# A masked prefix sum and a product: the last block comes last, in two parts, and is summed column group by column group

## The chip, the core and the metric

The kernel runs on one core of a Trainium2 chip. The metric is the device time of one execution in microseconds (us); smaller is better. TensorE multiplies matrices and writes to PSUM, VectorE and ScalarE work element by element, GpSimd fills tables, and SyncE and ScalarE issue the transfers between device memory and the on-chip memory (SBUF). Each engine has a queue of its own; semaphores tie them together.

## The reference

```
B, S, D = 8, 8192, 512
masked = x * (pos < lengths[:, None, None])
cs = np.cumsum(masked, axis=1)
mid_features = cs[arange(B), lengths // 2, :]
return matmul(mid_features[:, None, :], w).squeeze(1)
```

Only one row of each cumulative sum is used, so what is computed is, for each of the 8 sequences, the sum of its first n rows, n = min(length // 2 + 1, length), and then the product of the 8 sums (8x512) with w (512x512). Everything is float32. With the inputs drawn here n is 570, 2690, 256, 2057, 905, 3772, 3859 and 571 for sequences 0 to 7. In whole blocks of 512 rows that is 1, 5, 0, 4, 1, 7, 7 and 1 block, and a remainder of 58, 130, 256, 9, 393, 188, 275 and 59 rows. These are 26 blocks of 1 MB, some 3 MB of remainders, and 1 MB of w.

## The kernel before

**Tiling.** A block of 512 rows lies in SBUF as 128 partitions of four rows each (`(p g) d -> p g d`, 8 KB in one piece per partition). Four matmuls sum it: matmul j takes row j of every partition, and its weights (128 partitions by 8 columns) have ones in the column of the present sequence and zeros elsewhere. The four go to four column groups of the array, 32 columns apart, and each adds its 8 sums of 512 columns into partitions 32j to 32j+7 of the PSUM tile `s_ps`. In float32 each matmul shows as two records, so a block shows as eight.

**Stages.** VectorE first computes the row counts and a table of weights (`table`), in a chain of steps, each of which waits for the one before (`step`, L301 in the profile). Per sequence it copies that sequence's weights to `cur`. TensorE then goes through the sequences in pairs (`for q in range(2)`): it takes the weights and the remainder of the sequence (four matmuls), then its whole blocks (`add_block`). Ahead of each block but a sequence's first stand two bfloat16 matmuls into `idle_ps` (128x512), whose result nobody uses.

**Loads.** SyncE issues the whole blocks in order, into 6 buffers for even and 6 for odd sequences (`xt`, `NP = 6`). Before it fills a buffer again it waits until `s_sum`, which counts the sums made, has passed the one that last read it (`until`, L202). The very first block of sequence 0 goes to a tile of its own (`first`), before the lengths are known. ScalarE issues w and the remainders (`PARTS`: pieces of 256, 128, 64 rows and a last one of up to 64), into `rem`, one tile for even and one for odd sequences. `rem` has been zeroed by GpSimd (L289); ScalarE waits for that.

**End.** When all sums are made, VectorE copies `s_ps` to `s_sb` in two halves, ordered by column modulo 4 (L301, `s_sb<-s_ps`). Four matmuls with `fold` (L431) add the four groups and transpose at once: each takes 128 columns of `s_sb` as weights, and yields 128 columns of D on partitions by 8 sequences (`mf_ps`). Two copies bring them to `mf_sb`, and 16 matmuls multiply by w (L439) into `o_ps`. VectorE and ScalarE copy one half of the result each, and SyncE and ScalarE store them.

**Counts.** SyncE, ScalarE, VectorE and TensorE hold row counts in registers (`Counts`): they load the lengths from SBUF and compute with the queue's register instructions. Loops and conditions (`whole_blocks`, `Fori`, `If_cmp`) are branches on these engines' queues.

Of the kernel before, what the change touches and what calls it, by code (L numbers as in the profile page):

```python
# [16 lines left out]
def kernel(  # L17
# [15 lines left out]

    nc = tc.nc
# [5 lines left out]
    NP = 6  # L40
# [20 lines left out]
    def sem(name):  # L61
        return tc.alloc_semaphore(name)

    xt = sb("xt", [P, 2, NP, G, D])
    first = sb("first", [P, G, D])
# [3 lines left out]
    warm = sb("warm", [1, 1])  # L69
    n_i = sb("n_i", [1, B], I32)  # L70
    n_f = sb("n_f", [1, B])
    ones = sb("ones", [1, P])
    zb = sb("zb", [1, 32], BF16)
# [8 lines left out]
    first_w = sb("first_w", [P, B])  # L82
# [3 lines left out]
    zero = sb("zero", [1, D])  # L86
    fold_i = sb("fold_i", [P, B], I32)
    fold = sb("fold", [P, B])
    s_sb = sb("s_sb", [P, KC, P])
    mf_sb = sb("mf_sb", [P, KC, B])  # L90
# [3 lines left out]
    mf_ps = [ps(f"mf_ps{h}", [P, D]) for h in range(2)]  # L94
# [7 lines left out]
    s_w, s_first, s_len1, s_go, s_out = sem("w"), sem("first"), sem("len1"), sem("go"), sem("out")  # L102
# [7 lines left out]
    class Counts:  # L110


        def __init__(self, eng, ready, count, loaded=B):


            self.eng = eng
            self.raw = [eng.alloc_register(f"n_{eng.engine.name}_{i}") for i in range(2 * loaded)]
            self.regs = self.raw[::2]
            self.t = eng.alloc_register(f"t_{eng.engine.name}")
            eng.wait_ge(ready, count)  # L120
            eng.load(self.raw, lens1[:, :2 * loaded])
            self.pair = None
            if loaded < B:
                self.pair = eng.alloc_register(f"pair_{eng.engine.name}")
                eng.reg_mov(self.pair, 0)

        def without_first(self, base=None):

            alu, t, n = self.eng.reg_alu, self.t, self.rows(0)
            alu(t, n, 9, ALU.logical_shift_right)  # L130
            alu(t, t, 1, ALU.min)
            alu(t, t, 9, ALU.logical_shift_left)
            alu(n, n, t, ALU.subtract)
            if base is not None:
                alu(base, base, t, ALU.add)

            alu(n, n, 1, ALU.logical_shift_left)
            alu(n, n, 1, ALU.subtract)
            alu(n, n, 0, ALU.max)

        def rows(self, b):

            n = self.regs[b]
            self.eng.reg_alu(self.t, n, 1, ALU.logical_shift_right)
            self.eng.reg_alu(self.t, self.t, 1, ALU.add)
            self.eng.reg_alu(n, self.t, n, ALU.min)
            return n

        def next_pair(self):
            if self.pair is not None:  # L150

                self.eng.reg_alu(self.pair, self.pair, 4, ALU.add)
                self.eng.reg_alu(self.pair, self.pair, 2 * B - 4, ALU.min)
                self.eng.load(self.raw, lens1[:, ds(self.eng.snap(self.pair, min_val=0, max_val=2 * B - 4), 4)])
                return
            for to, of in zip(self.regs, self.regs[2:]):
                self.eng.reg_mov(to, of)

    def whole_blocks(eng, n, most, body, k=0):
# [5 lines left out]
    DVE_SEL, DVE_N, DVE_MASK = 2, 6, 28  # L165
# [6 lines left out]
        out=first[:], in_=xf[:BLK].rearrange("(p g) d -> p g d", g=G)  # L172
    ).then_inc(s_first, 16)
# [9 lines left out]
    def _(sp):  # L183
        ns = Counts(sp, s_len1, 16, loaded=2)
        sp.sem_inc(s_go, 1)
        base, at = sp.alloc_register("sp_base"), sp.alloc_register("sp_at")
        sp.reg_mov(base, 0)
        ns.without_first(base)

        items = sp.alloc_register("sp_items")  # L190
        sp.reg_mov(items, 2)
        until = [[sp.alloc_register(f"until{q}_{k}") for k in range(NP)] for q in range(2)]
        for u in until[0] + until[1]:
            sp.reg_mov(u, 1)
        with sp.Fori(0, B // 2):
            for q in range(2):
                n = ns.rows(q)
                sp.reg_alu(items, items, 1, ALU.add)

                def load_block(k):  # L200
                    sp.wait_ge(s_sum, until[q][k % NP])
# [275 lines left out]
```

## Time and profile before

| | |
|---|---|
| median of 14 runs | 88.89 us (87.97 to 89.81) |
| the profiled execution's own time | 88.54 us |
| its span, first to last instruction | 86.7 us |
| mean granted TensorE clock | 0.941 |
| moved by DMA | 31.29 MB, mean 361 GB/s |
| busy: TensorE matmuls, VectorE, ScalarE, GpSimd | 54.5, 10.6, 2.0, 4.4 us |
| issue of a whole block to its landing, median | 13.8 us |
| SyncE's waits for a sum before it fills a buffer again | 36.5 us in 10 waits |

The profile comes from one execution. Times in it count from the span's start; the 1.84 us between its span and its time lie outside. In a line of a timeline the columns are start, duration, engine (PE is TensorE, PEld its weight loads, DVE VectorE, ACT ScalarE, SPq SyncE's queue), line, operation, output <- inputs, shapes and count; in brackets the idle time of the engine before it and what ended that.

### The profile page before, as it was taken

To read this page: it belongs to the slowest core of one execution; us is meant where nothing else is said; L and a number is where in the kernel's file an instruction comes from. 1 tells how busy PE (TensorE), PEld (TensorE's weight loads), DVE (VectorE), ACT (ScalarE), POOL (GpSimd) and SP (SyncE) were. 2 spreads that over 40 slices of the span, in tenths; PEclk is the share of its full clock that TensorE was granted. 3 is DMA by queue.
4 is the path that set the end of the run, shared out by engine and by line. 5 is a ranking of instruction groups with operands and counts; after the bars stand their busy time and mean duration, and the time that the engine had idled before them with its cause. 6 is when DMAs were issued, how large, how long until landed. Compare 5 with 4: busy or idle time off the path is not lost. (4 is left out here: it accounts for less than half of the span.)

```text
span 86.7 us, 1383 instructions
## 1 busy us (share of the span) xinstructions
PE 54.5 (63%) x346; PEld 10.9 (13%) x350; DVE 10.6 (12%) x42; ACT 2.0 (2%) x4; POOL 4.4 (5%) x9
## 2 busy tenths in 40 slices
PE   0920251999994898059966199744995677448730
PEld 0220000121110211010200001100210011011520
DVE  3977600000000000000000000000000000000520
ACT  0000000000000000000004200000000000000020
POOL 5940000000000000000000000000000000000000
PEclk9999999999999999995799858997599999999999
DMA  2799999999999999999999999999999999990000
GB/s 30 321 408 291 374 404 423 416 431 423 419 415 420 423 419 419 416 396 424 423 419 417 417 425 423 423 423 423 423 416 416 423 423 423 423 389 15 0 0 11
DMA packets 4694, 31.29 MB, mean 361 GB/s; under 512 B 658, under 2 KB 674, under 8 KB 946
## 3 DMA queue, kind: packets, MB, share of 16 engines
q1 hardware_dynamic: 3762, 27.27, 76.7%
q10 hardware_dynamic: 928, 3.97, 11.8%
q14 instruction: 3, 0.02, 0.1%
q8 instruction: 1, 0.02, 0.1%
HBM read 31.23 MB, written 0.02 MB: 360 GB/s over the span
## 5 line engine op out<-in xcount | busy, mean ns | idle before, releaser
L381 PE MATMUL s_ps<-xt,cur 128*8 128x512 f32 x200 | 29.2, 650 | 14.8 <-PEq L108 14.7
L381 PE MATMUL s_ps<-rem,cur 128*8 128x512 f32 x64 | 12.3, 806 | 5.3 <-PEq L108 5.3
L415 PE MATMUL idle_ps<-idle 128*128 128x512 bf16 x30 | 9.8, 400 | 0.5 <-issue 0.3
L381 PEld LDWEIGHTS s_ps<-xt,cur 128*8 128x8 f32 x200 | 4.3, 90 | 30.4 <-issue 30.2
L355 DVE COPY cur<-table 128x40 f32<-128x40 f32 x8 | 1.4, 184 | 51.8 <-PE s_ps L381 51.8
L381 PE MATMUL s_ps<-first,first_w 128*8 128x512 f32 x8 | 1.9, 1042 | 4.0 <-DVE table L301 4.0
L415 PEld LDWEIGHTS idle_ps<-idle 128*128 128x128 bf16 x34 | 1.9, 98 | 15.6 <-issue 15.6
L381 PEld LDWEIGHTS s_ps<-rem,cur 128*8 128x8 f32 x64 | 1.8, 91 | 15.3 <-issue 15.2
L389 PE MATMUL s_ps<-zero 1*128 1x512 f32 x2 | 2.1, 1132 | 2.3 <-DVE ones L301 2.3
L289 POOL MEMSET rem<- 128x4096 f32 x1 | 3.5, 3511 | 0.0
L301 DVE COPY s_sb<-s_ps 128x256 f32<-128x256 f32 x2 | 0.8, 424 | 17.3 <-PE s_ps L381 17.3
L301 DVE TENSOR_SCALAR n_i<-lens 1x8 int32<-1x8 int32 x1 | 2.8, 2770 | 0.2 <-DMA lens<-in_lengths_dram 0.2
L275 ACT ACT_TABLE_LOAD x1 | 1.3, 1283 | 46.8 <-PE s_ps L381 46.8
L431 PE MATMUL mf_ps<-fold,s_sb 128*128 128x8 f32 x8 | 1.1, 260 | 0.5 <-DVE s_sb L301 0.5
L392 PE MATMUL n_ps<-n_f,ones 1*128 1x8 f32 x2 | 0.6, 368 | 1.2 <-DVE n_f L301 1.2
L278 ACT COPY o_sb<-o_ps 8x128 f32<-8x128 f32 x2 | 0.5, 258 | 35.0 <-PE o_ps L439 35.0
L431 PEld LDWEIGHTS mf_ps<-fold,s_sb 128*128 128x128 f32 x8 | 1.0, 190 | 1.5 <-DVE s_sb L301 1.5
L439 PE MATMUL o_ps<-wt,mf_sb 128*8 128x128 f32 x32 | 1.1, 273 | 0.0
L392 PEld LDWEIGHTS n_ps<-n_f,ones 1*128 1x128 f32 x2 | 0.5, 308 | 2.8 <-DVE n_f L301 2.8
L389 PEld LDWEIGHTS s_ps<-zero 1*128 1x128 f32 x2 | 0.5, 304 | 2.3 <-DVE ones L301 2.3
L439 PEld LDWEIGHTS o_ps<-wt,mf_sb 128*8 128x8 f32 x32 | 0.8, 89 | 0.0
L301 DVE COPY o_sb<-o_ps 8x128 f32<-8x128 f32 x2 | 0.6, 280 | 0.9 <-PE o_ps L439 0.8
(37 smaller groups left out, 6.7 us busy)
## 6 DMA issues: line engine op xcount, KB each, us to landing
xt<-in_x_dram SPq DMA_DIRECT2D x25, 1024.0 KB, 13.8
rem<-in_x_dram ACTq DMA_DIRECT2D x3, 512.0 KB, 7.1
wt<-in_w_dram ACTq DMA_DIRECT2D x1, 1024.0 KB, 6.4
first<-in_x_dram SPq DMA_DIRECT2D x1, 1024.0 KB, 8.2
rem<-in_x_dram ACTq DMA_DIRECT2D x3, 256.0 KB, 6.5
rem<-in_x_dram ACTq DMA_DIRECT2D x3, 128.0 KB, 6.5
rem<-in_x_dram ACTq DMA_DIRECT2D x3, 32.0 KB, 5.8
rem<-in_x_dram ACTq DMA_DIRECT2D x1, 64.0 KB, 6.2
```

The source lines that it names most:

```text
L275: act.copy(out=warm[:], in_=zero[:, :1])
L278: copy = act.copy(out=o_sb[1][:, j * P:(j + 1) * P], in_=o_ps[64 + 32 * j:64 + 32 * j + B, :P])
L289: pool.memset(rem[:], 0.0).then_inc(s_pool, 1)
L301: do(*args, **kw).then_inc(s_dve, 1)
L355: dve.tensor_copy(out=cur[:, b % 2], in_=table[:, b * WT:(b + 1) * WT]).then_inc(s_cur[b % 2], 1)
L381: return pe.matmul(s_ps[32 * j:32 * j + B], lhsT=weights, rhs=rows, start=False, stop=False, skip_group_check=True, tile_position=(0, 32 * j))
L389: pe.matmul(s_ps[:], lhsT=zero[:, :P], rhs=zero[:], start=True, stop=False, skip_group_check=True)
L392: pe.matmul(n_ps[:, :B], lhsT=ones[:], rhs=n_f[:], start=True, stop=True).then_inc(s_pe, 1)
L415: pe.matmul(idle_ps[:], lhsT=idle[:, :P], rhs=idle[:], start=True, stop=True)
L431: mm = pe.matmul(mf_ps[h][:, i * B:(i + 1) * B], lhsT=s_sb[:, 2 * h + i], rhs=fold[:], start=True, stop=True)
L439: mm = pe.matmul(o_ps[32 * j:32 * j + B, :P], lhsT=mf_sb[:, kc], rhs=wt[:, kc, j * P:(j + 1) * P], start=(kc == 0), stop=(kc == KC - 1), t ...
```

## The change

- **First block.** `first` is gone. Sequence 0's first block is loaded to the first of the `xt` buffers, still before the lengths are known, and is summed as that sequence's whole block, behind its remainder, with weights whose entry is zero where the sequence has fewer than 512 rows.
- **Last block.** If the last sequence has a whole block, its last one isn't among the blocks of the loop. SyncE issues it behind all others, into a tile `last` of its own and as two transfers, rows 0 and 1 and rows 2 and 3 of each partition, each with its own semaphore.
- **End.** After the loop `s_ps` is copied to `s_sb` as it stands, in two halves. Four matmuls with `fold` as weights (`add_column`) add the groups, matmul j for columns 128j to 128j+127, into partitions 32j to 32j+7 of `t_ps`. The last block is then added to the same tile: for each of its four rows four matmuls of 128 columns each. VectorE transposes `t_ps` in blocks of 32x32 into `t_sb`, in two instructions, and the product with w takes its weights from there.
- **Idle matmuls.** The pair (`keep_busy`) now also stands ahead of each sequence's remainder, ahead of the folds and ahead of the last block.
- **Buffers.** `NP` goes from 6 to 5.
- **Zeroing.** ScalarE zeroes the even half of `rem`, GpSimd the odd half, the latter once VectorE has made its tenth step. ScalarE's early `warm` copy, which came behind its loads, is gone.
- **Counts.** VectorE computes the rows per sequence for TensorE and itself into `blk_i` (five more steps); SyncE and ScalarE load the lengths by pairs (`Pairs`) and set their other registers before that.

```diff
-    NP = 6
+    NP = 5
...
-    class Counts:
+    class Pairs:
...
+        def step(self):
+
+            alu, top = self.eng.reg_alu, 2 * B - 4
+            alu(self.at, self.at, 4, ALU.add)
+            alu(self.at, self.at, top, ALU.min)
+            self.eng.load(self.raw, lens1[:, ds(self.eng.snap(self.at, min_val=0, max_val=top), 4)])
...
     nc.sync.dma_start(
-        out=first[:], in_=xf[:BLK].rearrange("(p g) d -> p g d", g=G)
-    ).then_inc(s_first, 16)
+        out=xt[:, 0, 0], in_=xf[:BLK].rearrange("(p g) d -> p g d", g=G)
+    ).then_inc(s_full[0][0], 16)
...
     @block.sync
...
+                    with sp.If_cmp(ns.at, 2 * B - 4, "IS_GE"):
+                        alu(has_last, n, 9, ALU.logical_shift_right)
+                        alu(has_last, has_last, 1, ALU.min)
+                        alu(last_at, has_last, 9, ALU.logical_shift_left)
+                        alu(n, n, last_at, ALU.subtract)
+                        alu(last_at, n, ~(BLK - 1), ALU.bitwise_and)
+                        alu(last_at, last_at, base, ALU.add)
...
+                def load_block(k):
+                    sp.wait_ge(s_sum, until[q][k % NP])
+                    alu(items, items, 1, ALU.add)
+                    sp.reg_mov(until[q][k % NP], items)
+                    if (q, k) == (0, 0):
+
+                        with sp.If_cmp(ns.at, 1, "IS_GE"):
+                            load(k)
+                    else:
+                        load(k)
...
+        with sp.If_cmp(has_last, 1, "IS_GE"):
+            from_rows = rows(sp, at, last_at, 0, BLK).rearrange("(p g) d -> p g d", g=G)
+            for h in range(2):
+                sp.dma_start(
+                    out=last[:, 2 * h:2 * h + 2], in_=from_rows[:, 2 * h:2 * h + 2]
+                ).then_inc(s_last[h], 16)
...
     @block.scalar
...
-        act.wait_ge(s_pool, 2)
+        act.memzero(rem[:, 0]).then_inc(s_zero[0], 1)
+        ns = Pairs(act, s_go, 1)
...
+                act.wait_ge(s_zero[q], 1)
                 act.wait_ge(s_sum, until[q])
...
-        act.wait_ge(s_dve, DVE_SEL)
-        act.copy(out=warm[:], in_=zero[:, :1])
...
-        pool.memset(rem[:], 0.0).then_inc(s_pool, 1)
         pool.memset(idle[:], 1.0).then_inc(s_pool, 1)
+        pool.wait_ge(s_dve, DVE_BLK)
+        pool.memset(rem[:, 1], 0.0).then_inc(s_zero[1], 1)
...
-        cols = s_ps[:].rearrange("p (i kc) -> p kc i", kc=KC)
         for h in range(2):
-            step(dve.tensor_copy, out=s_sb[:, 2 * h:2 * h + 2], in_=cols[:, 2 * h:2 * h + 2])
+            step(dve.tensor_copy, out=s_sb[:, 2 * P * h:2 * P * (h + 1)], in_=s_ps[:, 2 * P * h:2 * P * (h + 1)])
+        dve.wait_ge(s_pe, B + 3)
         for h in range(2):
-            dve.wait_ge(s_pe, B + 2 + h)
-            step(dve.tensor_copy, out=mf_sb[:, 2 * h:2 * h + 2].rearrange("p a b -> p (a b)"), in_=mf_ps[h][:, :2 * B])
+            step(dve.transpose, out=t_sb[:, 2 * h:2 * h + 2].rearrange("p k c -> p (k c)"),
+                 in_=t_ps[:, :P].rearrange("p (c k) -> p k c", k=KC)[:, 2 * h:2 * h + 2])
...
+        def keep_busy():
+
+            for _ in range(2):
+                pe.matmul(idle_ps[:], lhsT=idle[:, :P], rhs=idle[:], start=True, stop=True)
+
+        def add_column(j, weights, row, **kw):
+
+            return pe.matmul(t_ps[32 * j:32 * j + B, :P], lhsT=weights, rhs=row[:, P * j:P * (j + 1)],
+                             stop=False, skip_group_check=True, tile_position=(0, 32 * j), **kw)
...
-                pe.wait_ge(s_first, 16)
-                for j in range(G):
-                    mm = add(j, first_w[:], first[:, j])
-                mm.then_inc(s_sum, 1)
                 with pe.Fori(0, B // 2):
                     for q in range(2):
+                        keep_busy()
                         take(pe, s_cur[q], 1)
                         take(pe, s_rem[q], 16 * (len(PARTS) + 1))
...
-                for h in range(2):
-                    pe.wait_ge(s_dve, DVE_MASK + 1 + h)
-                    for i in range(2):
-                        mm = pe.matmul(mf_ps[h][:, i * B:(i + 1) * B], lhsT=s_sb[:, 2 * h + i],
-                                       rhs=fold[:], start=True, stop=True)
+                keep_busy()
+                for j in range(4):
+                    if j % 2 == 0:
+                        pe.wait_ge(s_dve, DVE_MASK + 1 + j // 2)
+                    mm = add_column(j, fold[:], s_sb, start=True)
+                mm.then_inc(s_pe, 1)
+                with pe.If_cmp(ns[B], 1, "IS_GE"):
+                    keep_busy()
+                    for g in range(G):
+                        if g % 2 == 0:
+                            pe.wait_ge(s_last[g // 2], 16)
+                        for j in range(4):
+                            mm = add_column(j, cur[:, 1, :B], last[:, g], start=False)
                     mm.then_inc(s_pe, 1)
+                with pe.Else():
+                    pe.sem_inc(s_pe, 1)
```

## The prediction

> **What bounds the kernel now.** I read the page's first two parts, then stretches of the span, then the timeline at both ends, then who waits for whom.
>
> ```profile
> span 86.7 us, 1383 instructions
> PE 54.5 (63%) x346; PEld 10.9 (13%) x350; DVE 10.6 (12%) x42; ACT 2.0 (2%) x4; POOL 4.4 (5%) x9
> DMA  2799999999999999999999999999999999990000
> ```
>
> Every compute engine has much idle time; the DMA row is at 9 from about 4 us to 78 us. The 31.29 MB are the bound, until the last slices, where nothing is moved any more. The columns of the next view are the stretch, its length, the busy time of the five engines, granted clock, DMA share, GB/s.
>
> ```profile
> 6.00:7.00 1.00, 0.21 (x2) 0.12 (x1) 0.52 (x7) 0.00 (x0) 0.00 (x0) 1.00 0.99 418
> 7.00:8.00 1.00, 0.00 (x0) 0.00 (x0) 0.83 (x6) 0.00 (x0) 0.00 (x0) 1.00 1.66 344
> 8.00:9.00 1.00, 0.00 (x0) 0.00 (x0) 0.83 (x6) 0.00 (x0) 0.00 (x0) 1.00 0.37 156
> 77.00:78.00 1.00, 0.90 (x9) 0.27 (x11) 0.00 (x0) 0.00 (x0) 0.00 (x0) 1.00 0.89 369
> 78.00:79.00 1.00, 1.00 (x12) 0.15 (x6) 0.00 (x0) 0.00 (x0) 0.00 (x0) 1.00 0.10 41
> ```
>
> The stream runs at about 420 GB/s, with one gap at 7 to 9 us, worth (420-344+420-156)/420 = 0.8 us: the 1 MB of `first` and of w are through, and the first block that SyncE issues after reading the lengths, at 5.08, isn't flowing yet. The end, from the timeline:
>
> ```profile
> 74.61 1.04 PE L381 MATMUL s_ps<-xt,cur 128*8 128x512 f32 x8 [0.90 <-PEq L108]
> 77.10 1.04 PE L381 MATMUL s_ps<-xt,cur 128*8 128x512 f32 x8 [1.45 <-PEq L108]
> 77.96 1.18 PE L381 MATMUL s_ps<-rem,cur 128*8 128x512 f32 x8
> 79.55 1.04 PE L381 MATMUL s_ps<-xt,cur 128*8 128x512 f32 x8 [0.41 <-PEq L108]
> 80.65 0.88 DVE L301 COPY s_sb<-s_ps 128x256 f32<-128x256 f32 x2 [17.25 <-PE s_ps L381]
> 81.13 1.07 PE L431 MATMUL mf_ps<-fold,s_sb 128*128 128x8 f32 x8 [0.54 <-DVE s_sb L301]
> 82.13 1.06 PE L439 MATMUL o_ps<-wt,mf_sb 128*8 128x128 f32 x32
> 83.26 0.59 DVE L301 COPY o_sb<-o_ps 8x128 f32<-8x128 f32 x2 [0.84 <-PE o_ps L439]
> ```
>
> At 77.10 TensorE sums the last block of sequence 6, at 77.96 the remainder of sequence 7, at 79.55 (0.14 after its landing, 13.8 us after issue at 65.58) the only whole block of sequence 7 (571 rows); then come copies, folds, product, copies. The start:
>
> ```profile
> 14.78 1.90 PE L381 MATMUL s_ps<-rem,cur 128*8 128x512 f32 x8 [2.66 <-PEq L108]
> 16.82 2.01 PE L381 MATMUL s_ps<-rem,cur 128*8 128x512 f32 x8 [0.15 <-PEq L108]
> 18.48 1.21 PE L381 MATMUL s_ps<-xt,cur 128*8 128x512 f32 x8
> 20.00 24.83 SPq L204 DMA_DIRECT2D xt<-in_x_dram  x12
> ```
>
> SyncE issues five blocks by 9.6, then needs a buffer whose sum ends at 19.69, and issues again at 20.00. The fifth of those blocks lands at 24.8 (15.6 after issue at 9.24); its data and the remainder beside it are through at about 23.5. So the stream is not broken there, but with little to spare.
>
> **The change part by part.** The profiled execution took 88.54 us: span 86.7 and 1.84 around it; the median is 88.89, 0.35 above. I add to the median.
>
> *Head, SyncE.* Some 16 register moves (0.05 each in the trace of its queue, 0.8) now stand ahead of the load of the lengths, which waited until 2.12 anyhow; moving from 1.7 to 2.6 it starts 0.4 late. Behind it 14 moves and the split of the first block go (0.9), a comparison, a branch taken past the load and more register work come in (0.4 to 0.5). The first block of sequence 1 is issued about 0.0 to 0.2 earlier than 5.08: nothing, bounds -0.3 and +0.3. The gap at 7 to 9 us stays.
>
> *Head, the zeroing of `rem`.* Half goes to ScalarE, behind its table load (1.28 in the row of L275). Its own price is not shown: the lower bound is ScalarE's copies, 0.19 for one column and 0.26 for 128, so 0.5 ns a column and 1.3 for 2048; the upper VectorE's slope, (424-175)/240 = 1.04 ns a column, 2.3. I take 1.76, half of GpSimd's row of 3.51, the same work. From 1.8 it ends at 1.8+1.28+1.76 = 4.85 (4.4 to 5.4); GpSimd's memset, which it replaces, ended at 4.87. So the first remainder is issued at about 6.65 and lands 8.0 later, as before. [...] The other half stays on GpSimd (1.76, behind VectorE's tenth step) and is needed at 7.9 only. VectorE's first read of the lengths took 2.77, ending with GpSimd's memset; that shrinks, five steps of 0.19 come in, but TensorE waits for the remainder until 14.7 either way: nothing.
>
> *Start, TensorE.* `first` was summed at 10.22 to 12.1, while the remainder was on its way. Now that block is summed behind the remainder, in time that counts, with two idle matmuls ahead of each remainder. At the slow clock a pass of four matmuls starts every 0.80, at the full one every 0.43 (the granted clock reads 1.00 all along here, so only the durations tell); the fast passes begin at 18.5, 3.7 after 14.78. From 14.78: remainder 1.60, block 1.60, idle 0.43+0.22 (the clock turns here), remainder 0.86, block of sequence 1 0.43+0.59: end at 20.5 instead of 19.69. SyncE issues at 20.8 to 20.9 instead of 20.00. Is the stream dry by then? The block issued at 5.08 into a stream about to end flowed at 7.66, 2.6 later, and cost a ramp of 0.8; by that row 20.9+2.6 = 23.5 against 23.4, so 0.1+0.8 = 0.9 lost. w's transfer, issued at 0.89, moved its first packet at 1.94, 1.05 later; by that row 22.0, and nothing is lost. I take 0.5, the middle, since each row has a defect (the first fell among other issues, the second met idle engines); bounds 0 and 0.9 in this clock phase. [...]
>
> *Buffers 12 to 10, plus `last`.* The sixth and seventh block of sequences 5 and 6 now wait for the sums of blocks 1 and 2 of the same sequence. Sequence 5's first block lands at 42.9 and is summed by 44.3; four blocks of 2.48 are then still on their way. `last` is issued behind sequence 6's seventh block, as two transfers (one more issue of 0.34 on SyncE's queue) at about 66.5 against 65.58, to land at 79.4. Hidden by 10 us of queued transfers; without that cover a block would cost up to 2.5.
>
> *End.* Count from L, the landing of sequence 6's last block (76.96 before). Before, o_sb starts at L+6.30. Now:
> - its sum starts at L+0.14. Two idle matmuls come ahead of the remainder (0.54; the step from one block to the next with them is 1.51): remainder from L+1.65 to L+2.69 (was to L+2.18).
> - copies to s_sb, 0.42 each: L+2.75 to L+3.63. TensorE's queue, after a sequence's last sum, needs 1.4 of branches and register work (79.59 to 81.01 before); from L+1.8 it is through at L+3.3, two idle matmuls then, so the folds (four of N=128, 0.22 as in the product) go at L+3.9.
> - a second pair of idle matmuls, with nothing to cover it, stands behind the folds: 0.54, `last` from L+4.7.
> - `last`'s halves land at L+1.3 to L+2.6: two microseconds earlier. So the wait on them costs nothing, and their split gains nothing. 16 matmuls of N=128: as the product, 1.06, to L+5.74.
> - transposes 128x64 out of PSUM: between the copy of 16 columns (0.175) and of 256 (0.42); by the slope 0.23. First to L+6.05, the second beside the product. Product 1.06 from L+6.17, o_sb at L+7.3.
>
> So +1.0. Bounds: +0.4 if the idle matmuls fit into the waits wholly (2 x 0.3), +1.5 if branches around the new condition add 0.2 twice and the transposes cost 0.42. The moved sum is shorter behind the landing, as the diff has it (0.14+0.6+0.3+1.1 against 3.85), but the landing no longer sets the end.
>
> Sum: 0.0 (head) + 0.5 (stream) + 1.0 (end) = +1.5: 90.0 for the profiled execution, 90.4 for the median.
>
> **The rivals.** *No second gap.* The stream holds and the end costs 0.6 to 1.0: 89.4 to 89.9. For it: 1.05 us of w's issue. Against: the ramp at 7 to 9 us.
>
> *Late clock.* If the clock turns only after sequence 1's first sum, the passes cost 1.60+1.60+0.85+1.60+1.60+0.25 = 7.5 from 14.78 instead of 5.75; SyncE issues at 22.6, the gap is 0.5+1.75, and with the end 88.89+1.0+2.2 = 92.1. For it: the times before spread by 1.8 us with nothing else to show for it. Against: before, the same clock served.
>
> *The landing of `last` sets the end.* Then the chain behind it is 2.2 instead of 3.85: -1.6, with the stream's 0 to 0.5 some 87.5. It decides once TensorE is ready for `last` by L+2.6, that is 2.1 earlier than I count; it begins to gain at L+3.7. For it: TensorE had 0.4 idle at 79.1 to 79.5. Against: six serial steps with durations from rows.
>
> **How the numbers follow.** Forecast 0.55 (89.5 to 91.3), no second gap 0.22, late clock 0.13, landing 0.10. A measurement here can't tell less than 0.5% (88.45 to 89.33) from no change: a third of the no-gap case and a little of the forecast's edge, 0.10; slower 0.80; faster 0.10. The range leaves out the landing case and the late clock's upper end: 88.9 to 91.9.
>
> **What would show it.** In the changed kernel's timeline: `last`'s matmuls start with no wait on its landing, some 2 us behind it; idle matmuls between folds and `last`; o_sb about 7.3 behind L. At the start: sequence 1's first sum ends near 20.5, and the GB/s row has a dip at 23 to 25 us. Wrong would be: `last` waited for at the queue, or a first remainder that lands well before 14.

## The result and the profile after

The changed kernel takes 89.68 us (median of 10 runs, 89.02 to 91.25), the kernel before 88.81 beside it (47 runs): a ratio of 1.0109, 95% interval 1.0077 to 1.0142. That is slower by 0.97 us (0.68 to 1.26). An execution more than 1.5% above the fastest of its kernel counts in the medians and ranges here, but not in the ratios and intervals.

The profiled execution took 88.99 us: span 87.2 and 1.8 around it, where the kernel before had 86.7 and 1.84. So the two profiles differ by 0.45 us, half of the loss. The other half lies where no profile has a row. Of the changed kernel 12 executions are on record with their spans: in 4 of them, the profiled one among these, 1.76 to 1.82 us lie outside the span, in the other 8 it is 2.15 to 2.58. Of the kernel before, beside the experiments below, all 72 executions have 1.75 to 1.85. Over the executions that the ratios count, the median span is 87.3 us for the changed kernel and 86.9 for the one before beside the experiments. So some 0.4 us of the loss are in the span and some 0.4 outside it. What the latter are no run shows; the account below is about the former.

The first two parts of the changed kernel's page:

```profile
span 87.2 us, 1472 instructions
PE 54.5 (62%) x391; PEld 10.8 (12%) x394; DVE 8.2 (9%) x45; ACT 3.7 (4%) x5; POOL 2.8 (3%) x9
DMA  2799999999999999999999999999999999970000
GB/s 30 316 428 350 354 403 411 437 425 425 417 406 413 421 425 417 428 391 428 428 421 410 421 421 421 421 421 421 421 421 421 421 421 421 415 291 0 0 0 11
```

As before, the stream fills the span until 78 us and then nothing is moved. No slice between 20 and 30 us (the tenth to the fourteenth) is below 406 GB/s, so the dip forecast for 23 to 25 us isn't there. The stretches that answer to those shown before (stretch, length, busy time of the five engines, granted clock, DMA share, GB/s):

```profile
6.00:7.00 1.00, 0.00 (x0) 0.00 (x0) 0.83 (x6) 0.00 (x0) 0.00 (x0) 1.00 0.95 401
7.00:8.00 1.00, 0.00 (x0) 0.00 (x0) 0.79 (x5) 0.00 (x0) 0.00 (x0) 1.00 1.30 344
8.00:9.00 1.00, 0.84 (x2) 0.14 (x2) 0.30 (x3) 0.00 (x0) 0.00 (x0) 1.00 0.75 319
77.00:78.00 1.00, 1.00 (x10) 0.11 (x2) 0.00 (x0) 0.00 (x0) 0.00 (x0) 1.00 0.81 324
78.00:79.00 1.00, 1.00 (x10) 0.12 (x8) 0.00 (x0) 0.00 (x0) 0.00 (x0) 1.00 0.06 25
```

The first gap got smaller: 319 GB/s at 8 to 9 us where it was 156, together (401+344+319-418-344-156)/420 = 0.35 us more data by 9 us. SyncE's first issue behind the lengths is at 4.74 instead of 5.08. The last block of sequence 6 lands at L = 76.51 instead of 76.96, so 0.45 us were gained by the stream in this execution. The end, from the timeline:

```profile
76.65 1.04 PE L403 MATMUL s_ps<-xt,cur 128*8 128x512 f32 x8 [0.91 <-PEq L113]
77.62 0.60 PE L410 MATMUL idle_ps<-idle 128*128 128x512 bf16 x2
78.16 1.04 PE L403 MATMUL s_ps<-rem,cur 128*8 128x512 f32 x8
79.14 0.60 PE L410 MATMUL idle_ps<-idle 128*128 128x512 bf16 x2
79.30 0.88 DVE L319 COPY s_sb<-s_ps 128x256 f32<-128x256 f32 x2 [17.24 <-PE s_ps L403]
79.78 0.85 PE L414 MATMUL t_ps<-s_sb,fold 128*8 128x128 f32 x8
80.56 0.60 PE L410 MATMUL idle_ps<-idle 128*128 128x512 bf16 x2
81.09 1.06 PE L414 MATMUL t_ps<-last,cur 128*8 128x128 f32 x32
82.22 0.53 DVE L319 STREAM_TRANSPOSE t_sb<-t_ps 128x64 f32<-128x64 f32 x2 [2.04 <-PE t_ps L414]
82.62 1.06 PE L478 MATMUL o_ps<-wt,t_sb 128*8 128x128 f32 x32 [0.47 <-DVE t_sb L319]
83.74 0.59 DVE L319 COPY o_sb<-o_ps 8x128 f32<-8x128 f32 x2 [0.98 <-PE o_ps L478]
```

From L to the copy of the result it is 83.74-76.51 = 7.23 us; before it was 6.30. The end is 0.93 us longer, and since L comes 0.45 earlier, the span grows by half of that. The matmuls of `last` stand at 81.09 with no idle time in brackets; the two transfers into `last` landed at 77.79 and 79.00, the second of them 2.1 us earlier. TensorE walks from one item to the next through the remainder, the folds and `last`, with an idle pair ahead of each. The start (weight loads left out):

```profile
14.12 1.89 PE L403 MATMUL s_ps<-rem,cur 128*8 128x512 f32 x8 [4.95 <-PEq L113]
...
15.78 1.94 PE L403 MATMUL s_ps<-xt,cur 128*8 128x512 f32 x8
...
17.65 0.75 PE L410 MATMUL idle_ps<-idle 128*128 128x512 bf16 x2
...
18.34 1.04 PE L403 MATMUL s_ps<-rem,cur 128*8 128x512 f32 x8
...
19.20 1.04 PE L403 MATMUL s_ps<-xt,cur 128*8 128x512 f32 x8
...
20.56 0.34 SPq L203 DMA_DIRECT2D xt<-in_x_dram  x1
```

The order of the prediction is there: remainder, block, idle pair, remainder, block, and then SyncE's reissue (its next issue, into a freed buffer). It comes at 20.56 instead of 20.00, less late than the 20.8 to 20.9 that was forecast, since the first remainder landed at 13.99 instead of 14.64.

### The profile page after: what moved, and what is told of

Same layout as the page of the kernel before. It is cut to its first block, busy times and chain, and to the rows that moved or that the text cites. A ratio compares the mean times of both kernels' runs of the same rounds, so it can differ in the third digit from the quotient of the medians.

```text
span 87.2 us, 1472 instructions
## 1 busy us (share of the span) xinstructions
PE 54.5 (62%) x391; PEld 10.8 (12%) x394; DVE 8.2 (9%) x45; ACT 3.7 (4%) x5; POOL 2.8 (3%) x9
## 5 line engine op out<-in xcount | busy, mean ns | idle before, releaser
L403 PE MATMUL s_ps<-xt,cur 128*8 128x512 f32 x200 | 27.0, 612 | 16.6 <-PEq L113 16.6
L410 PE MATMUL idle_ps<-idle 128*128 128x512 bf16 x51 | 16.2, 396 | 4.8 <-DVE table L319 3.5
L403 PE MATMUL s_ps<-rem,cur 128*8 128x512 f32 x64 | 9.2, 650 | 5.0 <-PEq L113 5.0
L410 PEld LDWEIGHTS idle_ps<-idle 128*128 128x128 bf16 x54 | 3.1, 97 | 27.1 <-issue 27.1
L403 PEld LDWEIGHTS s_ps<-rem,cur 128*8 128x8 f32 x64 | 1.0, 87 | 8.9 <-issue 8.9
L244 ACT ACTIVATE rem<-rem 128x2048 uint32<-128x2048 uint32 x1 | 1.9, 1910 | 0.0
L308 POOL MEMSET rem<- 128x2048 f32 x1 | 1.8, 1805 | 1.7 <-DVE blk_i L319 1.7
L478 PE MATMUL o_ps<-wt,t_sb 128*8 128x128 f32 x32 | 1.1, 273 | 0.5 <-DVE t_sb L319 0.5
L414 PE MATMUL t_ps<-last,cur 128*8 128x128 f32 x32 | 1.1, 273 | 0.0
L478 PEld LDWEIGHTS o_ps<-wt,t_sb 128*8 128x8 f32 x32 | 0.8, 89 | 0.7 <-issue 0.7
```

The costliest lines, as they stand in the source:

```text
L244: act.memzero(rem[:, 0]).then_inc(s_zero[0], 1)
L308: pool.memset(rem[:, 1], 0.0).then_inc(s_zero[1], 1)
L403: return pe.matmul(s_ps[32 * j:32 * j + B], lhsT=weights, rhs=rows, start=False, stop=False, skip_group_check=True, tile_position=(0, 32 * j))
L410: pe.matmul(idle_ps[:], lhsT=idle[:, :P], rhs=idle[:], start=True, stop=True)
L414: return pe.matmul(t_ps[32 * j:32 * j + B, :P], lhsT=weights, rhs=row[:, P * j:P * (j + 1)], stop=False, skip_group_check=True, tile_posit ...
L478: mm = pe.matmul(o_ps[32 * j:32 * j + B, :P], lhsT=t_sb[:, kc, :B], rhs=wt[:, kc, j * P:(j + 1) * P], start=(kc == 0), stop=(kc == KC - 1) ...
```

## The experiments

The theory at this point was: the whole loss is the chain of serial work behind L on TensorE, its idle pairs above all, and the landing of `last` decides nothing; further, the stream has a second gap only where SyncE's reissue comes late. The rivals were that the ring of five buffers or the place of `last` in the stream costs the time, and that the clock does. The letters in the expectations are told there. The ratios are to the kernel before on the same chip, with 95% intervals. The changed kernel was not run again beside them, so what is said against it compares ratios, or spans. "The end" is the time from L to the copy of the result.

**One idle pair out.** The pair ahead of the last block:

```diff
                 with pe.If_cmp(ns[B], 1, "IS_GE"):
-                    keep_busy()
                     for g in range(G):
```

> The changed kernel without the idle pair ahead of the last block. Counting from L, the landing of sequence 6's last block. Theory A (the end on TensorE costs the time): the last block's matmuls start 0.54 earlier, at L+4.05, and the output copies at L+6.7 instead of L+7.23; 0.54 us faster than the changed kernel, 0.4 slower than the kernel before. Rival B (the stream at the start and the ten buffers cost the time, the idle pairs only fill waits): no difference to the changed kernel. Rival C (the pair holds the clock): the passes of the last block or of the product go slow, 1 us or more is added.

It took 88.95 us (12 runs), ratio 0.9983 (0.9934 to 1.0031): level with the kernel before, and below the changed kernel's interval. Its timeline:

```profile
80.97 0.85 PE L414 MATMUL t_ps<-s_sb,fold 128*8 128x128 f32 x8
...
81.56 1.14 PE L414 MATMUL t_ps<-last,cur 128*8 128x128 f32 x32
...
84.26 0.59 DVE L319 COPY o_sb<-o_ps 8x128 f32<-8x128 f32 x2 [0.98 <-PE o_ps L477]
```

The second half of the folds runs straight into `last`; with L at 77.71 the end is 6.55, 0.68 shorter than in the changed kernel. Two matmuls that compute nothing, in series with everything, cost 0.68 of the 0.93 us by which the end had grown. Against the changed kernel's ratio this run is 1.1 us faster, twice the 0.54 expected. Its median span (86.8 us, over the executions that the ratio counts) is 0.5 below the changed kernel's 87.3, as expected; the rest is time outside the span, 1.76 to 1.85 us in all 12 executions here.

**The pairs ahead of the remainders out as well.**

```diff
                     for q in range(2):
-                        keep_busy()
                         take(pe, s_cur[q], 1)
```

> The changed kernel without the idle pairs ahead of the last block and ahead of every remainder; the pair ahead of the folds and those between blocks stay. A: the output copies at L+6.15, 1.1 us faster than the changed kernel, 0.1 faster than the kernel before. B: no difference to the changed kernel, apart from the first sum of sequence 1, which comes some 0.6 earlier. C: slow passes at the end, 1 us or more.

It took 88.12 us (12 runs), ratio 0.9916 (0.9873 to 0.9958), but the end didn't get shorter: L = 76.33, result copy at 82.85, 6.52 instead of the 6.15 expected. TensorE's timeline of this kernel:

```profile
73.97 1.81 PE L403 MATMUL s_ps<-xt,cur 128*8 128x512 f32 x8 [1.44 <-PEq L113]
75.71 1.04 PE L410 MATMUL idle_ps<-idle 128*128 128x512 bf16 x2
76.68 1.44 PE L403 MATMUL s_ps<-xt,cur 128*8 128x512 f32 x8
77.95 1.03 PE L403 MATMUL s_ps<-rem,cur 128*8 128x512 f32 x8
```

Its granted clock, by stretches:

```profile
73.00:74.00 1.00, 0.03 (x4) 0.06 (x8) 0.00 (x0) 0.00 (x0) 0.00 (x0) 1.00 0.94 393
74.00:75.00 1.00, 1.00 (x8) 0.09 (x8) 0.00 (x0) 0.00 (x0) 0.00 (x0) 0.56 0.99 406
75.00:76.00 1.00, 1.00 (x5) 0.13 (x2) 0.00 (x0) 0.00 (x0) 0.00 (x0) 0.50 1.01 406
```

The clock was at 0.50 to 0.56 from 74 to 77 us, so the passes of sequence 6's last two blocks and the idle pair took up to 1.7 times as long, and the block that landed at 76.33 waited for the idle pair ahead of it until 76.68. Whether the pairs that were taken out had held the clock is not settled: the profile of the kernel before has such stretches too, at 40 to 42, 50 to 52 and 60 to 62 us (0.50 in each), with the stream at 433, 415 and 422 GB/s there. If the time is better than in the run before (the two intervals overlap), that doesn't come from the end.

**`last` back in the loop.** The condition that takes the last block out never holds; all else is the changed kernel.

```diff
-                        alu(has_last, n, 9, ALU.logical_shift_right)
+                        alu(has_last, n, 30, ALU.logical_shift_right)
...
-        step(dve.tensor_scalar, out=cut[:], in0=n_f[:, B - 1:], scalar1=BLK, scalar2=None, op0=ALU.is_ge)
+        step(dve.tensor_scalar, out=cut[:], in0=n_f[:, B - 1:], scalar1=S, scalar2=None, op0=ALU.is_ge)
```

> The changed kernel with the last sequence's block back in the loop, in a buffer of the ring and summed like the others; folds, transposes, idle pairs and the start as in the changed kernel. A: the block's sum starts 0.14 behind its landing at L+2.45, then copies, folds and transposes follow it in series: output copies at L+6.6, 0.65 us faster than the changed kernel although everything now stands behind the last landing, 0.3 slower than the kernel before. B: as the changed kernel within 0.2.

It took 88.72 us (12 runs), ratio 0.9987 (0.9947 to 1.0027); L to the result copy 76.57 to 83.25 = 6.68. The moved sum is therefore no gain by itself: with the block where it had been, the same transposes and folds are 0.55 us faster at the end. Rival B falls.

**Remainders first.** Both remainders of a pair of sequences are summed ahead of the pair's blocks, so that none stands between sequence 6's last block and the end; the idle pair ahead of `last` is out, the one ahead of the folds stays.

```diff
                 with pe.Fori(0, B // 2):
+                    keep_busy()
                     for q in range(2):
-                        keep_busy()
                         take(pe, s_cur[q], 1)
...
+                    for q in range(2):
+                        if q:
+                            pe.matmul(idle_ps[:], lhsT=idle[:, :P], rhs=idle[:], start=True, stop=True).then_inc(s_pe, 1)
                         n = ns[q]
...
-                    keep_busy()
                     for g in range(G):
```

> The changed kernel with both remainders of a pair of sequences summed ahead of the pair's blocks, and without the idle pair ahead of the last block. Nothing but copies and folds then stands between sequence 6's last sum and the last block. A: TensorE is ready for the last block at L+2.6, the last half lands at L+2.5, so the landing sets the end: output copies at L+4.8, 2.4 us faster than the changed kernel, 1.5 faster than the kernel before. B: no difference to the changed kernel at the end; the start sets the time.

It took 87.97 us (6 runs), ratio 0.9891 (0.9823 to 0.9959). The end: L = 76.74, result copy at 82.39, so 5.65 instead of the 4.8 expected. Where the 0.85 are, from its timeline:

```profile
77.98 0.88 DVE L323 COPY s_sb<-s_ps 128x256 f32<-128x256 f32 x2 [15.51 <-PE s_ps L407]
...
79.00 0.60 PE L414 MATMUL idle_ps<-idle 128*128 128x512 bf16 x2 [0.75 <-issue]
...
79.53 0.41 PE L418 MATMUL t_ps<-s_sb,fold 128*8 128x128 f32 x8
...
79.75 1.06 PE L418 MATMUL t_ps<-last,cur 128*8 128x128 f32 x32
```

The copies are through at 78.86, but the idle pair starts only at 79.00, after 0.75 us in which TensorE waited for nothing but its own queue (branches and register work of the loop), and holds the folds until 79.53. With the remainder out of the way the queue, which was hidden in the changed kernel, and the pair show.

**The same with a short queue.** The rolled loop over blocks becomes eight nested conditions, and the pair ahead of the folds goes.

```diff
-                        with pe.Fori(0, -(-NB // NP)):
-                            whole_blocks(pe, n, NP, add_block)
-                            pe.reg_alu(n, n, NP * BLK, ALU.subtract)
-                            pe.reg_alu(n, n, 0, ALU.max)
+                        whole_blocks(pe, n, NB, add_block)
...
-                keep_busy()
                 for j in range(4):
```

> As the kernel with the remainders first, and two things less on TensorE's queue at the end: the block loop is one chain of up to eight conditions instead of two rounds of five, so that a sequence without blocks costs one branch, and the idle pair ahead of the folds is gone. In the kernel with the remainders first the folds waited for the queue until 2.8 us behind L, though both copies were made at L+2.1. Theory D (branches and register work on TensorE's queue set the end there): folds at L+2.2, the last block's second half at its landing, L+2.5, output copies at L+4.85 instead of L+5.65, 0.8 us faster, some 1.8 faster than the kernel before. Rival E (something else, the copies or the landing, sets it): output copies at L+5.4 or later.

The end was 5.01 (79.06 to 84.07), near the 4.85 expected, but the time was 89.2 us (12 runs; 88.67 for the seven that the ratio counts), ratio 0.9981 (0.9929 to 1.0032), where 1.8 us less than before was expected. What the end gained was lost earlier: in the profiled execution (89.41 us) TensorE's first matmul came at 7.64 us instead of 2.33, and SyncE's reissue at 22.93. That was not foreseen; it is taken up below.

**First block early.** The same, and sequence 0's first block is summed ahead of the loop, as before the change, straight from the weights in `table`.

```diff
+                take(pe, s_full[0][0], 16)
+                for j in range(G):
+                    mm = add(j, table[:, :B], xt[:, 0, 0, j])
+                mm.then_inc(s_sum, 1)
                 with pe.Fori(0, B // 2):
```

> As the kernel with the short queue, and sequence 0's first block is summed ahead of the loop, while the first remainder is on its way, as the kernel before does. Theory F (a second gap opens in the stream where SyncE's next issue comes later than about 20.5): the next issue comes at 19.5 to 20.0, the GB/s row has no dip between 22 and 28 us, and the time is 0.3 to 0.9 us below that of the kernel with the short queue, whose next issue comes at about 21. Rival G (the dips there come from the small transfers of remainders, not from the issue): the dip stays and the times are the same.

It took 87.88 us (6 runs), ratio 0.9892 (0.9835 to 0.9948), end 5.01 again. The reissue came at 20.66, later than expected, because the first remainder, issued at the usual 6.5 us, landed at 15.21. The dip didn't go (385 GB/s from 20 to 30 us), so this run doesn't decide between F and G.

**A later first sum.** The changed kernel with eight idle matmuls ahead of sequence 1's remainder, in the first round only.

```diff
+                        if q:
+                            with pe.If(pair < 1):
+                                for _ in range(4):
+                                    keep_busy()
                         keep_busy()
```

> The changed kernel with eight more idle matmuls ahead of sequence 1's remainder, in the first round of the loop alone. SyncE's next issue comes about 2 us later, at 22.5 instead of 20.56. F: the stream breaks, the GB/s row shows a dip of 1.5 to 2 us at 22 to 27 us, and L and the time move by as much: 91.2 to 91.7. Rival H (the issue has slack until 22.3, as w's first transfer, 1.05 us from issue to data, would have it): at most 0.4 us slower than the changed kernel.

It took 93.67 us (4 runs), ratio 1.0574 (1.0494 to 1.0654). The end was 7.23 as in the changed kernel; the loss is in the stream. The rates by slice, of 2.28 us each:

```profile
GB/s 29 342 418 421 406 363 426 415 421 367 65 303 331 414 411 429 425 418 420 427 421 421 424 418 419 421 421 425 421 421 421 425 418 418 407 209 4 0 0 18
```

SyncE's reissue came at 24.07 instead of the 22.5 expected, and the tenth to thirteenth slice are the second gap of the prediction, one that the changed kernel itself does not have. Rival H falls; the time is 2 us above what F expected. Part of the delay came from a late first remainder (14.85), so this run has two causes in it.

**Six buffers.** The changed kernel with `NP = 6`.

> The changed kernel with six buffers per parity instead of five. All theories but B: within 0.2 us of the changed kernel, since the fifth buffer is refilled some 10 us ahead of need. B (the smaller ring costs the time): 0.5 to 1 us faster than the changed kernel.

It took 92.04 us (5 runs), ratio 1.0379 (1.0317 to 1.0441): 2.4 us above the changed kernel, with one buffer more. A miss for every theory. Its end was 7.23, its reissue at 22.19.

**The length of TensorE's program.** The runs with the unrolled loop, the eight idle matmuls and the six buffers have two things in common: TensorE's program is longer (118 to 145 matmuls are written out in it, against 110 in the changed kernel and 102 in the one before), and the first matmul is late. So: the changed kernel, with 14 matmuls behind the product that are never executed.

```diff
+                with pe.If_cmp(ns[B], 2, "IS_GE"):
+                    for _ in range(14):
+                        pe.matmul(idle_ps[:], lhsT=idle[:, :P], rhs=idle[:], start=True, stop=True)
```

> The changed kernel with 14 matmuls more in TensorE's program, behind the product, under a condition that never holds: nothing more is executed, the program is as long as that of the run with six buffers, and the ring stays at five. In four runs (unrolled loop twice, eight idle matmuls more, six buffers) TensorE's first matmul came at 7.6 us instead of 2.3, and the instruction queue q8 moved 5 packets instead of 1. Theory S, the program's length does this: first matmul at 7.6, q8 at 5 packets, the first block's data released some 2 us later, time 92.0 (91.3 to 92.7) as with six buffers. Theory R, the sixth buffer itself cost 2.4 us there and the late first matmul is a consequence of nothing in the program's length: first matmul at 2.3, q8 at 1 packet, time as the changed kernel, 89.7 (89.2 to 90.2). The end is the same in both, o_sb 7.2 us behind the landing of the last block.

It took 91.06 us (4 runs), ratio 1.0235 (1.0152 to 1.0317), above the changed kernel's interval and a little under what was expected of the length alone. Its profile is of the slowest of its executions, 91.88 us; the first matmul is as late in the profiles of the four runs before. TensorE's first entry in the changed kernel's timeline:

```profile
2.33 2.06 PE L421 MATMUL s_ps<-zero 1*128 1x512 f32 x2 [2.33 <-DVE n_i L319]
```

and in that of the kernel with unused code:

```profile
7.68 2.06 PE L421 MATMUL s_ps<-zero 1*128 1x512 f32 x2 [7.68 <-DVE fold L319]
```

The instruction queues in the third part of the changed kernel's page (packets, MB, share of 16 engines):

```profile
q8 instruction: 1, 0.02, 0.1%
```

and of the one with unused code:

```profile
q8 instruction: 5, 0.08, 0.5%
```

What TensorE did until then is in the rows of L419, `with pe.If(i >= 1)`: in the first of two turns this branch jumps over the whole body. In the changed kernel (shortest, median and longest in ns, start of the first and the last in us):

```profile
L419 PEldq COMPARE_BRANCH  x2: 69/212/356, 1.2 to 2.2; - x2
```

and with the unused code:

```profile
L419 PEldq COMPARE_BRANCH  x2: 69/2800/5532, 1.2 to 7.6; - x2
```

The jump over the body took 5.53 us instead of 0.36 (5.49 with six buffers). Code that never runs moved the first matmul by 5.3 us and brought four more packets of instructions (five of 0.08 MB together instead of one of 0.02); so the length does it, not the work. In these kernels the border lies between 110 and 118 matmuls: in nine profiles with up to 110 the first matmul comes at 2.3 us, in five with 118 or more at 7.6 to 7.8. One of the five packets came between 4 and 5 us, while TensorE stood in this branch, and the next two between 10 and 12; but the changed kernel's only packet came between 4 and 5 us as well. What the branch waited for isn't shown.

The late first matmul is covered by itself: with six buffers the weights were ready at 11.1 and the first remainder was still on its way. What reaches the stream is that this remainder lands late. In the profiles of the nine kernels of this study with a short program it landed at 13.39 to 14.64; in the five with a long one at 14.85 to 16.69, while its issue stayed at 6.5. Why landings come late there isn't shown. Nor is all of the six buffers' loss explained: 2.7 points of the ratio lie between them and the changed kernel, 1.3 of them with unused code, and the two intervals touch.

**The kernel before with five buffers.** The ring alone, from the other side.

```diff
-    NP = 6
+    NP = 5
```

> The kernel before, with five buffers a slot in place of six; nothing else is edited. In the runs with the edit's end, six buffers were slower than five, and unused code alone was slower too. Theory S (the length of TensorE's program did that, and the ring itself costs nothing either way): the first reissue at 20.0 and the landing at 77.0 as before, first matmul at 2.3, o_sb 6.3 us behind the landing, time as before within 0.4 us: 88.9 (88.5 to 89.3). Theory R (five buffers are better for the stream than six, by what the run with six lost beyond the run with unused code, about 1 us): faster than before by 0.6 us or more. Rival W (the sixth and seventh block of a long sequence wait in the ring): slower by 0.5 us or more, with a slice under 390 GB/s at 40 to 60 us.

It took 88.61 us (12 runs), ratio 0.9982 (0.9947 to 1.0017), reissue at 19.53, first matmul at 2.33. Five buffers cost nothing and gain nothing; both rivals fall.

**A short program and no idle pair at the end.** Remainders first, without the pair ahead of the folds, the loop rolled.

> The kernel with the remainders first and no idle pair before the last block, with the idle pair before the folds taken out as well; the loop stays rolled, so TensorE's program is short. With the loop unrolled this end took 5.01 us from the landing to o_sb, but TensorE began late and the time was 89.2. Theory S (the length cost it): first matmul at 2.3, o_sb at the landing plus 5.0 (4.9 to 5.4), landing at 76.7 as with the remainders first, time 87.97 - 0.6 = 87.4 (86.9 to 87.9). Rival Q, TensorE's queue branches of the rolled loop are still late without the pair (the pair began at 79.00 there, behind an issue of 0.75): o_sb at the landing plus 5.5 or more, time 87.8 to 88.0.

The first matmul came at 2.3 us, and the end was 5.11 (77.82 to 82.93): the branches of the rolled loop cost 0.1 at most, and rival Q falls. The second half of `last` landed at 80.33, when the matmuls of its first half had just begun (80.29) and before its own were due: even here the landing doesn't set the end, but by now it is close to doing so. But the time was 88.2 us (5 runs), ratio 0.9899 (0.9809 to 0.9989), no better than with the pair and above the 86.9 to 87.9 expected. TensorE's timeline of the start:

```profile
16.54 1.90 PE L407 MATMUL s_ps<-rem,cur 128*8 128x512 f32 x8 [0.76 <-PEq L113]
18.20 1.94 PE L407 MATMUL s_ps<-xt,cur 128*8 128x512 f32 x8
20.08 0.61 PE L446 MATMUL idle_ps<-idle 128*128 128x512 bf16 x1
20.62 1.90 PE L407 MATMUL s_ps<-xt,cur 128*8 128x512 f32 x8
22.45 0.60 PE L414 MATMUL idle_ps<-idle 128*128 128x512 bf16 x2
22.98 1.04 PE L407 MATMUL s_ps<-xt,cur 128*8 128x512 f32 x8
```

and its stretches:

```profile
22.00:23.00 1.00, 1.00 (x9) 0.14 (x8) 0.00 (x0) 0.00 (x0) 0.00 (x0) 1.00 0.44 174
23.00:24.00 1.00, 1.00 (x10) 0.14 (x10) 0.00 (x0) 0.00 (x0) 0.00 (x0) 1.00 0.66 121
24.00:25.00 1.00, 1.00 (x14) 0.18 (x10) 0.00 (x0) 0.00 (x0) 0.00 (x0) 1.00 0.44 123
```

Every pass (the eight records of four matmuls) up to 22.4 takes 1.9 us, the prediction's slow clock, where the changed kernel's take 1.04 from 18.34. The moment isn't the same with the same start either: with one idle pair out the fast passes begin at 19.10. SyncE's reissue slips to 22.83, and for three microseconds the stream runs at a third. This is the prediction's rival of the late clock, in a sister kernel: (420x3-174-121-123)/420 = 2.0 us. The clock in the profile's rows reads 1.00 all through, so only the durations tell.

**And the first block early.** The same, with sequence 0's first block summed ahead of the loop.

> The kernel of the run before, and sequence 0's first block is summed ahead of the loop, still rolled. Theory F with S (the reissue decides on a second gap, and TensorE starts in time): first matmul at 2.3, SyncE's reissue at 20.0 or earlier, no slice under 390 GB/s between 21 and 26 us, landing at 76.2, time 86.9 (86.4 to 87.4). Rival N (with the remainders first the stream has no gap worth more than 0.2 us any more): the same as the run before within 0.3 us.

It took 87.35 us (5 runs, 86.79 to 88.88), ratio 0.9811 (0.9738 to 0.9884), the fastest of all kernels here. Its rates by slice, of 2.13 us each:

```profile
GB/s 8 315 423 427 423 403 407 429 419 427 427 388 427 427 427 411 419 419 404 423 419 428 408 417 431 427 423 415 419 427 411 431 427 423 407 404 104 0 0 12
```

That is within what theory F with S expected (86.4 to 87.4). TensorE starts at 2.33, the block is summed at 9.87 in time that was idle, the reissue comes at 19.93 and the stream has no gap; the end is 5.15 (76.64 to 81.79). It beats the kernel before by 1.68 us (1.03 to 2.33), and the end's 6.30-5.15 = 1.15 account for most of that. Against the run before the intervals overlap, so the gain of the early block in the median isn't separated from noise; the stream shows it.

The profiles side by side, by the time of SyncE's reissue. The data lost is (420 - rate)/420 of the ten microseconds from 20 to 30:

| kernel | SyncE's reissue | GB/s, 20 to 30 us | lost, us |
|---|---|---|---|
| before, five buffers | 19.53 | 418 | 0.0 |
| first block early, rolled | 19.93 | 415 | 0.1 |
| before | 20.00 | 419 | 0.0 |
| idle pairs ahead of remainders out | 20.50 | 416 | 0.1 |
| the changed kernel | 20.56 | 415 | 0.1 |
| first block early, unrolled | 20.66 | 385 | 0.8 |
| `last` in the loop | 20.68 | 411 | 0.2 |
| remainders first | 21.00 | 379 | 1.0 |
| one idle pair out | 21.32 | 408 | 0.3 |
| six buffers | 22.19 | 365 | 1.3 |
| remainders first, no pair | 22.83 | 332 | 2.1 |
| short queue, unrolled (execution of 89.41 us) | 22.93 | 319 | 2.4 |
| unused code (execution of 91.88 us) | 23.09 | 340 | 1.9 |
| later first sum | 24.07 | 280 | 3.3 |

With a short program a reissue up to 20.7 costs next to nothing; past 21 the loss grows with the delay, by 2.0 us from 22.19 to 24.07. The one early reissue that lost 0.8 belongs to a long program, with its late landings. The edge isn't sharp (0.3 lost at 21.32, 1.0 at 21.00), and the changed kernel stood some tenths from it.

## Why the prediction was right, and where not

The forecast was 90.4 us, slower than before; 89.68 was measured, inside the range. The end, its largest term, was right. That the sum is near is partly luck: head and stream were put at +0.5 together and gave -0.45 in the profile, and a term that the sum doesn't have, time outside the span, gave some +0.4. By its own steps:

- **Head, SyncE, 0.0: mis-sized.** The first issue came 0.34 earlier, just past the bound of 0.3, and shrank the first gap by 0.35 us in this execution, most of the 0.45 by which L comes earlier. "The gap stays" was not so.
- **Head, the zeroing: right.** ScalarE's half took 1.91 us, where 1.76 was taken, and ended at 4.82 against 4.85 forecast. It began at 2.91, right behind the table load, which took 1.28 and ended at 2.90. GpSimd's half took 1.81 and was never waited for.
- **Start and stream, +0.5: mis-sized.** This step failed in two places. The first remainder landed 0.65 earlier than the kernel before had it, so the reissue came at 20.56, not 20.8 to 20.9, although the passes up to it took 0.4 longer than counted (14.12 to 20.24 instead of 14.78 to 20.5). And the price of a late reissue was set as the middle of two rows; the runs show that up to 20.7 it is next to nothing, and that where the stream does run dry the rate rises again 1.0 us behind the issue (22.83 to 23.81, and 24.07 to 25.06), the row of w's transfer and not the 2.6 of the other. In the changed kernel's profile 0.1 us is lost from 20 to 30 us. So what happened is the first rival, no second gap, and 89.68 lies within its 89.4 to 89.9 as well as in the forecast's own range. The late-clock rival did not show in the changed kernel (passes of 1.04 us from 18.34), but its slow passes did in the run with the reissue at 22.83 (1.9 us each up to 22.4).
- **Buffers 12 to 10 plus `last`: right for its reason.** The ring alone is worth nothing (0.9982, 0.9947 to 1.0017), and `last` landed at L+1.28 and L+2.49, forecast L+1.3 to L+2.6. What the step didn't see is that the smaller `NP` also keeps TensorE's program short, which has a price of its own (`NP = 6` took 92.04 us, not all of it by the length).
- **End, +1.0: right at +0.93, partly by two errors that cancel.** The folds were put at L+3.9, behind 1.4 us of branches on TensorE's queue and the idle pair. They began at L+3.27: the queue's branches ran during the matmuls of the remainder and the pair ran during the copies. But their second half waited for the second copy, so they took 0.85 where 0.22 was counted, and `last` began at L+4.58 against L+4.7. From there all is as forecast: 1.06 for `last`, 0.25 per transpose (0.23 taken), result copy at L+7.23 (7.3 forecast). That the landing of `last` would not decide is confirmed, by the trace and by putting the block back into the loop.
- **Outside the span: left out.** The 1.84 us around the span were carried over without a reason. They were 2.15 to 2.58 in 8 of the changed kernel's 12 executions, and 1.79 to 2.15 in the five of the fastest kernel above; in the other runs they stayed at 1.75 to 1.94. The cause is open.

## What to carry to other kernels

Here moving work behind the last transfer paid only once the engine that does it was ready at about the time of the landing (end of 5.1 us, against 6.3 before and 7.2 in the changed kernel). So count what stands in series on that engine from the last thing that is late, keep-busy matmuls included, before counting what lies behind the landing. In these runs the buffer that is refilled first had a deadline, which can be read from the trace (some 20.7 to 21 us): a later release within it cost next to nothing, and past it the loss grew about as fast as the delay. Where a program grows by unrolling or by more buffers, look at the time of the engine's first instruction (here a first matmul at 2.3 us with up to 110 matmuls written out, at 7.6 to 7.8 with 118 or more), at the branch before it and at the packets of its instruction queue. And compare spans as well as times: what lies outside the span has no row in a profile.

## What was unexpected in the hardware

- Fourteen matmuls that never run cost 1.1 us by the ratios (1.0235 against 1.0109) and 1.7 by the median spans of the executions that these count (89.0 against 87.3): a branch over the body of 5.53 us instead of 0.36, first matmul at 7.68 instead of 2.33, and 5 packets on the instruction queue instead of 1. With six buffers, where the program is as long, the first remainder landed 1.9 us later at an unchanged issue (15.85 against 13.99).
- The same four matmuls took 1.9 us instead of 1.04, as late as 22.4 us into one kernel, while the granted clock in the stretches read 1.00. At 74 us of another kernel they took 1.81 with a granted clock of 0.50 to 0.56 in the row. That the early ones are a slow clock too is read from the durations alone.
- In the kernel before, VectorE's first read of the lengths took 2.77 us beside GpSimd's memset; in the changed kernel VectorE's small operations at 4.78 to 5.35 took 0.15 each beside a memset of the same kind (3.60 to 5.41). What held the first was not tried.
